# Modulation sums of two half-matrices kept in one PSUM bank, gathered by small DMAs and turned by one transpose per vector

## The chip, the core and the metric

The kernel runs on one core of a Trainium2 chip. The core has TensorE (matrix products, PE in the profile), VectorE (DVE), ScalarE (ACT), GpSimd (POOL) and SyncE (SP), an on-chip memory of 128 partitions (SBUF) and a smaller one of eight banks into which TensorE writes (PSUM). Transfers are issued by an engine's queue and carried out by 16 DMA engines. The metric is the time of one execution in microseconds of the device. Three runs of the kernel before gave 1747.1, 1747.19 and 1747.67 us, a median of 1747.19.

## The reference

Two layers of a network on 512 rows of width 1024, in 32-bit floats. Each layer has a mixer (layer 0: a gated recurrence beside gated linear attention; layer 1: a gated delta rule) and a mixture of 32 experts. Around both stands a modulation computed from one vector `c`:

```python
cond = jax.nn.silu(c)
for layer in range(DEPTH):
    mod = cond @ w_ada[layer] + b_ada[layer]
    sh1, sc1, gt1, sh2, sc2, gt2 = jnp.split(mod[:, None, :], 6, axis=-1)
    u = rms_norm(h, norm1[layer]) * (1.0 + sc1) + sh1
    h = h + gt1 * mixer(u)
    u = rms_norm(h, norm2[layer]) * (1.0 + sc2) + sh2
    h = h + gt2 * hier_moe(u, ...)
```

So each layer needs six vectors of 1024 numbers (v = 0 to 5 in the kernel: sh1, sc1, gt1, sh2, sc2, gt2). Each is a product of a vector of 1024 with a matrix of 1024 x 1024, 4 MB of `w_ada`. Vectors 1 and 4 are further increased by one and multiplied with the norm's weights.

## The kernel before

The kernel runs through four stages: the mixer of layer 0 (to about 290 us), its experts (to about 810 us), the mixer of layer 1 (to about 1235 us) and its experts. In the mixers TensorE multiplies weights that ScalarE has split into a high part (`whi`) and GpSimd into a low part (`wlo`), three products for each pair of operands (lines 402 to 404). In the experts, pairs of experts go through TensorE, their weights (1 MB a transfer, issued by SP) in a ring of buffers.

Two vectors of layer 0 (0 and 1) are made at the start by other code, which the change does not touch. The other ten come from `mods` (line 302): six in layer 0's mixer, among them vectors 1 and 0 of layer 1, and four in layer 1's. `mods` is a generator that runs beside the mixer: the class `Stream` counts steps of the mixer's loop, and each `yield n` lets n steps pass (`M0 = 3, 4, 4` steps in layer 0, `M1 = 6` in layer 1). So the modulation's instructions are written between those of the mixer. A scheduler then fixes the order on each engine, mostly as written, and gives the tiles their room and the semaphores.

The matrix of a vector is taken in quarters: two halves of the columns (`hb`), and in each two halves of the rows (`i`), each a transfer of 1 MB by SP. `mod_rows` (line 254) multiplies one quarter: four matmuls, each with one column of `cond` repeated 32 times, write to the four groups of 32 partitions of a PSUM bank, so that each group holds a part of the sum, the same in its 32 rows. ScalarE copies the bank to `modrow` for `i` = 0 (line 337), VectorE adds the bank for `i` = 1 to it (line 333). One step later `finish` makes columns of it: `mod_columns` (line 261) multiplies each of four blocks of 128 columns with a column of `fold`, which adds the four partial sums and puts the result on 128 partitions. That is four matmuls of one column with a weight load of 128 each, twice per vector. `mod_finish` (line 289) adds the bias and, for vectors 1 and 4, the norm's weights, on VectorE. For vectors 3 and 4 the columns are taken in an interleaved order (`spread`, line 42).

Vectors are used as columns in `u_block` (line 519), in the router's product with `wr` (line 1260, started through `then` when vector 3 is done) and by `gate_rows` (line 347). In order of creation the vectors of layer 0's mixer are (0, 2), (0, 4), (0, 3), (0, 5), (1, 1), (1, 0), written as (layer, v); those of layer 1's are (1, 2), (1, 4), (1, 3), (1, 5).

Eight PSUM banks serve all products (`ps`, line 116). The queue of SP issues every transfer of the middle of the program; ScalarE issues three at the start and two at the end.

Of the kernel before, what the change touches and what calls it, by code (L numbers as in the profile page):

```python
# [7 lines left out]
F32 = mybir.dt.float32  # L8
# [4 lines left out]
OP = mybir.AluOpType  # L13
AX = mybir.AxisListType
# [3 lines left out]
P = 128  # L18
# [23 lines left out]
def spread(x, h):  # L42

    return [x[:, c + j:c + 256:2] for c in (512 * h, 512 * h + 256) for j in range(2)]
# [45 lines left out]
class Build:  # L90
# [167 lines left out]
            self.nc.tensor.matmul(p[32 * q:32 * q + 32], self.cond[:, k0 + q:k0 + q + 1].to_broadcast([P, 32]), w[:, q],  # L258
                                  start=start, stop=stop)

    def mod_columns(self, p, rows, spaced=False):

        for j in range(4):
            x = spread(rows, 0)[j] if spaced else rows[:, j * P:(j + 1) * P]
            self.nc.tensor.matmul(p[:, j:j + 1], x, self.fold[:, 0:1], start=True, stop=True)

    def mod_first(self, hb, p):
        nc = self.nc
# [17 lines left out]
                             stop=True)  # L286
        yield p

    def mod_finish(self, l, v, hb, p):

        nc = self.nc
        d = self.mod_vec(l, v)[:, 4 * hb:4 * hb + 4]
        spaced = v in (3, 4)
        b = self.spc[:, :, 4 * l + 2 * (v - 3) + hb] if spaced else self.C("bada", 48 * l + 8 * v + 4 * hb, 4)
        nc.vector.tensor_add(d, p, b)
        if v % 3 == 1:
            g = self.spc[:, :, 8 + 2 * l + hb] if spaced else self.C("norm1", 8 * l + 4 * hb, 4)
            nc.vector.scalar_tensor_tensor(d, d, 1.0, g, op0=OP.add, op1=OP.mult)
        if hb:
            self.ready.add((l, v))  # L300

    def mods(self, vs, pool, ahead, pace, then={}):


        seq = [(l, v, hb, i) for l, v in vs for hb in range(2) for i in range(2)]
        tiles = []

        def issue():
            if len(tiles) < len(seq):
                l, v, hb, i = seq[len(tiles)]  # L310
                src = self.a["w_ada"][l][512 * i:512 * i + 512, v * D + hb * 512:v * D + hb * 512 + 512]
                tiles.append(self.load(src, 512, pool))

        def finish():
            _, l, v, hb, rows = made.pop(0)
            p = self.ps([P, 4])
            self.mod_columns(p, rows, v in (3, 4))
            self.mod_finish(l, v, hb, p)
            if hb and (l, v) in then:
                then[l, v]()  # L320
        for _ in range(ahead):
            issue()
        made = []
        for n, (l, v, hb, i) in enumerate(seq):
            yield pace[n % len(pace)]
            if made and made[0][0] == n:
                finish()
            p = self.ps()
            self.mod_rows(p, tiles[n], 4 * i)
            tiles[n] = None  # L330
            issue()
            if i:
                self.nc.vector.tensor_add(rows, rows, p)
                made.append((n + 1, l, v, hb, rows))
            else:
                rows = self.mix.tile([P, 512], F32, name="modrow", tag="modrow")
                self.nc.scalar.activation(rows, p, AF.Copy)
        for _ in range(len(made)):
            yield 3
            finish()  # L340

    def get(self, l, v):

# [1616 lines left out]
```

## Time and profile before

| | |
|---|---|
| median of three runs | 1747.19 us |
| profiled execution | 1746.73 us, span 1745.0 us |
| mean granted TensorE clock | 0.973 |
| PE busy | 1651.2 us (95%), 9036 records |
| DVE busy | 806.4 us (46%) |
| ACT busy | 518.9 us (30%) |
| POOL busy | 394.8 us (23%) |

The span runs from the first to the last instruction. Busy time is the time in which an engine has at least one instruction in work; TensorE's matmuls overlap, and a 32-bit product of 512 columns has two records. A matmul's weight load has its own line (PEld). The granted clock is 1.0 at TensorE's full speed and 0.5 at half. The time in square brackets behind a row is the engine's idle time just before it, with what ended it.

### The profile page before, as it was taken

The page shows a single profiled execution, that of the slowest core. Times are in us where ns is not written, and L with a number is a line of the kernel's source. Part 1 is how long each engine was busy: PE and PEld are TensorE (multiplying, and loading weights), DVE is VectorE, ACT ScalarE, POOL GpSimd, SP SyncE. Part 2 cuts the span into 40 slices and gives each one's busy share as a digit, 9 for nine tenths or more (in the row PEclk, how much of TensorE's full clock was granted, in tenths as well). Part 3 has the DMA queues.
Part 4 walks back from the last instruction along what each step waited for, and adds up shares of the span by engine and source line. Part 5 has one row for each costly group of instructions (what it writes and reads, how often), then busy time and mean ns, then how long its engine had stood idle before and what let it go on. Part 6 is the DMA issues. An engine that isn't in the chain of part 4 may idle for free. (4 is left out here: it accounts for less than half of the span.)

```text
span 1745.0 us, 23263 instructions
## 1 busy us (share of the span) xinstructions
PE 1651.2 (95%) x9036; PEld 1003.2 (57%) x9036; DVE 806.4 (46%) x1793; ACT 518.9 (30%) x1027; POOL 394.8 (23%) x350
## 2 busy tenths in 40 slices
PE   6999999899999999998988989899999999999996
PEld 3666767544554555454667667678544554555453
DVE  2344653532433233335687787865432433243324
ACT  4745332310110111014636475364310110111013
POOL 2443523210010101001534343353210010101011
PEclk9999999999999999998999999999999999999998
DMA  8655655589999999994243432237599999999992
GB/s 300 223 173 175 217 185 216 221 358 380 413 413 412 413 411 414 411 409 137 63 141 111 132 110 85 85 106 281 226 368 378 413 411 412 413 411 414 412 407 106
DMA packets 156051, 495.89 MB, mean 284 GB/s; under 512 B 16216, under 2 KB 43156, under 8 KB 140576
## 3 DMA queue, kind: packets, MB, share of 16 engines
q1 hardware_dynamic: 155488, 493.23, 73.4%
q8 instruction: 74, 1.21, 0.3%
q10 hardware_dynamic: 448, 1.11, 0.2%
q14 instruction: 41, 0.34, 0.1%
HBM read 492.21 MB, written 2.10 MB: 283 GB/s over the span
## 5 line engine op out<-in xcount | busy, mean ns | idle before, releaser
L1502 PE MATMUL ps<-w,XTm 128*64 128x512 f32 x2048 | 447.2, 593 | 0.0
L1502 PEld LDWEIGHTS ps<-w,XTm 128*64 128x64 f32 x2048 | 161.7, 137 | 267.6 <-issue 260.7
L396 POOL TENSOR_TENSOR wlo<-w,whi 128x512 fp32r<-128x512 f32 x136 | 181.5, 1339 | 269.1 <-ACT whi L395 251.4
L1556 PE MATMUL ps<-w,hT 128*64 128x512 f32 (+1 forms) x1056 | 230.9, 587 | 1.0 <-ACT hT L1534 1.0
L1525 DVE TENSOR_TENSOR gg<-gg,ps 128x512 f32<-128x512 f32 x32 | 22.0, 688 | 377.4 <-PE ps L1502 377.3
L402 PE MATMUL ps<-w,whi 128*128 128x512 f32 x384 | 165.6, 432 | 0.0
L403 PE MATMUL ps<-w,whi 128*128 128x512 f32 x384 | 155.2, 405 | 2.1 <-POOL w L526 1.5
L1556 PEld LDWEIGHTS ps<-w,hT 128*64 128x64 f32 x1056 | 82.2, 137 | 130.2 <-issue 117.5
L404 PE MATMUL ps<-w,wlo 128*128 128x512 f32 x384 | 155.4, 405 | 0.0
L1579 DVE TENSOR_TENSOR w<-w,ps 128x512 f32<-128x512 f32 (+1 forms) x248 | 149.4, 665 | 7.0 <-PE ps L1570 5.5
L1511 POOL CAST sel<-ident 32x128 fp32r<-32x128 f32 x32 | 9.0, 280 | 591.7 <-PE ps L1539 533.9
L1560 POOL TENSOR_TENSOR yl<-y,yh 128x512 fp32r<-128x512 f32 x60 | 76.4, 1274 | 251.3 <-ACT yh L1559 251.3
L1559 ACT ACTIVATE yh<-y 128x512 fp32r<-128x512 f32 (+1 forms) x66 | 40.8, 618 | 295.4 <-DVE y L1558 294.4
L395 ACT ACTIVATE whi<-w 128x512 fp32r<-128x512 f32 x136 | 84.4, 627 | 147.5 <-PE ps L403 81.0
L1426 PE MATMUL ps<-Dm,hhi 128*128 128x256 f32 x512 | 126.2, 288 | 0.0
L1426 PE MATMUL ps<-Dm,hlo 128*128 128x256 f32 x512 | 123.6, 284 | 0.0
L1558 DVE SCALAR_TENSOR_TENSOR y<-ps,wsl,gate 128x512 f32<-128x512 f32 (+1 forms) x66 | 48.5, 735 | 151.5 <-issue 76.3
L1426 PEld LDWEIGHTS ps<-Dm,hhi 128*128 128x128 f32 x512 | 101.5, 199 | 13.4 <-issue 13.3
L1570 PE MATMUL ps<-yh,dt 128*128 128x512 f32 (+1 forms) x264 | 106.0, 406 | 0.0
L1534 ACT ACTIVATE hT<-ps 128x512 f32<-128x512 f32 x32 | 19.1, 598 | 284.2 <-PE ps L1532 265.9
L1426 PEld LDWEIGHTS ps<-Dm,hlo 128*128 128x128 f32 x512 | 101.6, 199 | 0.1
L1570 PE MATMUL ps<-yl,dt 128*128 128x512 f32 (+1 forms) x264 | 100.9, 387 | 0.0
(520 smaller groups left out, 2433.4 us busy)
## 6 DMA issues: line engine op xcount, KB each, us to landing
w<-in_moe_w_dram SPq DMA_DIRECT2D x380, 1024.0 KB, 14.9
w<-in_w_ada_dram SPq DMA_DIRECT2D x40, 1024.0 KB, 5.5
w<-in_w_in_c_dram SPq DMA_DIRECT2D x16, 1024.0 KB, 9.0
w<-in_w_in_ab_dram SPq DMA_DIRECT2D x10, 1024.0 KB
wst<-in_w_ada_dram SPq DMA_DIRECT2D x8, 1024.0 KB, 12.9
w<-in_w_out_ab_dram SPq DMA_DIRECT2D x4, 1024.0 KB, 4.8
w<-in_moe_w_dram SPq DMA_DIRECT2D x8, 512.0 KB, 15.2
w<-in_w_out_c_dram SPq DMA_DIRECT2D x4, 1024.0 KB, 4.9
```

What stands on the lines that cost most here:

```text
L395: nc.scalar.activation(hi, src, AF.Copy)
L396: nc.gpsimd.tensor_sub(lo, src, hi.bitcast(F32))
L402: mm(p, lhs[0], rhs[0], start=start, stop=False)
L403: mm(p, lhs[0], rhs[1], start=False, stop=False)
L404: mm(p, lhs[1], rhs[0], start=False, stop=stop)
L1426: nc.tensor.matmul(p, spread(src[:, t], k // 4)[k % 4], Dm[:, t].rearrange("p e s -> p (e s)"), start=t + i == 0, stop=t == NT - 1 and i == 1)
L1502: self.nc.tensor.matmul(ps[j][half[e]], X[:, k, half[e]], w, start=k == 0, stop=k == KD - 1)
L1556: nc.tensor.matmul(py[half[e]], hT[:, k, half[e]], w, start=k == 0, stop=k == 3)
L1558: nc.vector.scalar_tensor_tensor(y32, py, wsl, gate[:, c], op0=OP.mult, op1=OP.mult)
L1560: (nc.vector if last else nc.gpsimd).tensor_sub(yl[:, c], y32, yh[:, c].bitcast(F32))
L1570: mm = nc.tensor.matmul(p, dt[:, t * P:(t + 1) * P], y[:, s], start=i == 0, stop=i == 1)
L1579: nc.vector.tensor_add(h, h, p)
```

## The change

The sums of both row halves of a column half are now formed in one PSUM bank: `mod_rows` for `i` = 0 starts the bank and for `i` = 1 goes on in it, so the bank is held over one step of the generator, and VectorE's addition is gone. ScalarE copies the bank to `modrow` once, after `i` = 1. Only four of the 128 rows of `modrow` differ (rows 0, 32, 64 and 96). Small transfers, issued by ScalarE, carry these four rows in pieces into a small tile `modst`: 32 rows of 128 numbers for most vectors (four transfers per half), 16 rows of 256 for vectors 3 and 4 (two per half). When both halves are there, one transpose on TensorE (two for vectors 3 and 4) puts the pieces on 128 partitions, one VectorE reduction adds the four partial sums of all eight columns, and the bias and norm operations run once per vector instead of once per half. `finish` is written after the next vector's first `mod_rows`, and what hangs on a finished vector (`then`) one step of the generator later. The number of modulation matmuls and of 1 MB transfers stays.

```diff
@@ -258,11 +258,10 @@
             self.nc.tensor.matmul(p[32 * q:32 * q + 32], self.cond[:, k0 + q:k0 + q + 1].to_broadcast([P, 32]), w[:, q],
                                   start=start, stop=stop)
 
-    def mod_columns(self, p, rows, spaced=False):
+    def mod_columns(self, p, rows):
 
         for j in range(4):
-            x = spread(rows, 0)[j] if spaced else rows[:, j * P:(j + 1) * P]
-            self.nc.tensor.matmul(p[:, j:j + 1], x, self.fold[:, 0:1], start=True, stop=True)
+            self.nc.tensor.matmul(p[:, j:j + 1], rows[:, j * P:(j + 1) * P], self.fold[:, 0:1], start=True, stop=True)
 
     def mod_first(self, hb, p):
         nc = self.nc
@@ -286,18 +285,32 @@
                              stop=True)
         yield p
 
-    def mod_finish(self, l, v, hb, p):
+    def mod_finish(self, l, v, st):
 
         nc = self.nc
-        d = self.mod_vec(l, v)[:, 4 * hb:4 * hb + 4]
-        spaced = v in (3, 4)
-        b = self.spc[:, :, 4 * l + 2 * (v - 3) + hb] if spaced else self.C("bada", 48 * l + 8 * v + 4 * hb, 4)
-        nc.vector.tensor_add(d, p, b)
+        d = self.mod_vec(l, v)
+        n = st.shape[0]
+        if v in (3, 4):
+            p = self.ps([P, 2, n])
+            for j in range(2):
+                nc.tensor.transpose(p[:, j], st[:, j::2], self.ident[:n, :n])
+            src = p.rearrange("p j (h c q) -> p h c j q", h=2, q=4)
+            dst = d.rearrange("p (h c j) -> p h c j", h=2, c=2)
+            b = self.spc[:, :, 4 * l + 2 * (v - 3):4 * l + 2 * (v - 3) + 2].rearrange("p a h -> p h a")
+            g = self.spc[:, :, 8 + 2 * l:8 + 2 * l + 2].rearrange("p a h -> p h a")
+        else:
+            p = self.ps([P, n])
+            nc.tensor.transpose(p, st, self.ident[:n, :n])
+            src = p.rearrange("p (h j q) -> p h j q", h=2, q=4)
+            dst = d.rearrange("p (h j) -> p h j", h=2)
+            b = self.C("bada", 48 * l + 8 * v, 8).rearrange("p (h a) -> p h a", h=2)
+            g = self.C("norm1", 8 * l, 8).rearrange("p (h a) -> p h a", h=2)
+        nc.vector.tensor_reduce(dst, src, axis=AX.X, op=OP.add)
+        d = d.rearrange("p (h a) -> p h a", h=2)
+        nc.vector.tensor_add(d, d, b)
         if v % 3 == 1:
-            g = self.spc[:, :, 8 + 2 * l + hb] if spaced else self.C("norm1", 8 * l + 4 * hb, 4)
             nc.vector.scalar_tensor_tensor(d, d, 1.0, g, op0=OP.add, op1=OP.mult)
-        if hb:
-            self.ready.add((l, v))
+        self.ready.add((l, v))
 
     def mods(self, vs, pool, ahead, pace, then={}):
 
@@ -312,32 +325,47 @@
                 tiles.append(self.load(src, 512, pool))
 
         def finish():
-            _, l, v, hb, rows = made.pop(0)
-            p = self.ps([P, 4])
-            self.mod_columns(p, rows, v in (3, 4))
-            self.mod_finish(l, v, hb, p)
-            if hb and (l, v) in then:
-                then[l, v]()
+            _, l, v, st = made.pop(0)
+            self.mod_finish(l, v, st)
+            if (l, v) in then:
+                after.append(then[l, v])
         for _ in range(ahead):
             issue()
-        made = []
+        made, after = [], []
         for n, (l, v, hb, i) in enumerate(seq):
             yield pace[n % len(pace)]
-            if made and made[0][0] == n:
-                finish()
-            p = self.ps()
-            self.mod_rows(p, tiles[n], 4 * i)
+            if not i:
+                p = self.ps()
+            self.mod_rows(p, tiles[n], 4 * i, not i, i == 1)
             tiles[n] = None
             issue()
+            while after:
+                after.pop()()
+            if made and made[0][0] < n:
+                finish()
             if i:
-                self.nc.vector.tensor_add(rows, rows, p)
-                made.append((n + 1, l, v, hb, rows))
-            else:
                 rows = self.mix.tile([P, 512], F32, name="modrow", tag="modrow")
                 self.nc.scalar.activation(rows, p, AF.Copy)
+                if not hb:
+                    st = self.mod_stack(v)
+
+                m, w = st.shape
+                for j in range(m // 8):
+                    r = m // 2 * hb + 4 * j
+                    self.nc.scalar.dma_start(st[r:r + 4], rows[::32, w * j:w * j + w])
+                if hb:
+                    made.append((n, l, v, st))
         for _ in range(len(made)):
+            yield 4
+            finish()
+        while after:
             yield 3
-            finish()
+            after.pop()()
+
+    def mod_stack(self, v):
+
+
+        return self.mix.tile([16, 256] if v in (3, 4) else [32, P], F32, name="modst%d" % (v in (3, 4)), bufs=1)
 
     def get(self, l, v):
```

On ScalarE, in layer 0's mixer (`modrow` is the copied bank, `modst` the gathered rows, `whi` the high part of mixer weights), it stands so before:

```order
L592 ACTIVATE xc<-ps,cv_167 128x512
L337 ACTIVATE modrow<-ps 128x512
L395 ACTIVATE whi<-w 128x512 x2
L629 ACTIVATE ge<-ps 128x512
L635 ACT_TABLE_LOAD
L635 ACTIVATE ge<-ge 128x512
L337 ACTIVATE modrow<-ps 128x512
```

and now:

```order
L620 ACTIVATE xc<-ps,cv_167 128x512
L348 ACTIVATE modrow<-ps 128x512
L355 DMA modst_600<-modrow 4x128 x4
L423 ACTIVATE whi<-w 128x512 x2
L657 ACTIVATE ge<-ps 128x512
L663 ACT_TABLE_LOAD
L663 ACTIVATE ge<-ge 128x512
```

Four transfers stand behind each copy, ahead of the next weight split; a copy per half has moved, and none is added.

On TensorE at vector (0, 3) and the router's product (`mod_1054`, in the new kernel `mod_1209`, is that vector; `wr` the router's weights; `w,cond` modulation matmuls), before:

```order
L402 MATMUL ps<-w,whi 128x512
L403 MATMUL ps<-w,whi 128x512
L404 MATMUL ps<-w,wlo 128x512
L265 MATMUL ps<-fold,modrow 128x1 x4
L1260 MATMUL ps<-wr,mod_1054 128x36 x4
L258 MATMUL ps<-w,cond 32x512 x4
L402 MATMUL ps<-w,whi 128x512
L1260 MATMUL ps<-wr,mod_1054 128x36 x4
L403 MATMUL ps<-w,whi 128x512
L404 MATMUL ps<-w,wlo 128x512
```

and now (between the pieces stand 15 matmuls of the mixer):

```order
L258 MATMUL ps<-w,cond 32x512
L296 MATMUL ps<-ident,modst_1009 128x16 x2
L430 MATMUL ps<-w,whi 128x512
L431 MATMUL ps<-w,whi 128x512
L432 MATMUL ps<-w,wlo 128x512
...
L432 MATMUL ps<-w,wlo 128x512
L258 MATMUL ps<-w,cond 32x512 x3
L1288 MATMUL ps<-wr,mod_1209 128x36 x8
L430 MATMUL ps<-w,whi 128x512
```

The column matmuls are replaced by two transposes, and the router's product has moved behind the next modulation matmuls.

On TensorE at the last vector of layer 0's mixer, (1, 0), before (`orow` is the attention's output, `whi` and `yBhi` the output projection):

```order
L404 MATMUL ps<-whi,yAlo 128x512
L258 MATMUL ps<-w,cond 32x512 x4
L883 MATMUL ps<-ident,orow 128x128 x4
L265 MATMUL ps<-fold,modrow 128x1 x4
L402 MATMUL ps<-whi,yBhi 128x512
```

and now:

```order
L432 MATMUL ps<-whi,yAlo 128x512
L258 MATMUL ps<-w,cond 32x512 x4
L911 MATMUL ps<-ident,orow 128x128 x4
L303 MATMUL ps<-ident,modst_1936 128x32
L430 MATMUL ps<-whi,yBhi 128x512
```

Four column matmuls have become one transpose; the distance to the modulation matmuls is the same.

## Rows read from the trace of the kernel before

**Rows 1.** Stages: us; busy (count) of PE, PEld, DVE, ACT, POOL; PEclk; DMA; GB/s.

```profile
0.00:44.00 44.00, 27.67 (x163) 15.70 (x164) 13.06 (x37) 17.63 (x26) 10.93 (x17) 1.00 0.83 298
44.00:290.00 246.00, 237.02 (x1215) 165.65 (x1214) 118.46 (x228) 112.85 (x223) 104.59 (x75) 0.94 0.59 202
330.00:780.00 450.00, 448.38 (x2298) 229.82 (x2298) 148.15 (x272) 54.98 (x91) 40.14 (x44) 1.00 0.99 398
830.00:1200.00 370.00, 337.41 (x2235) 258.81 (x2234) 284.50 (x756) 200.46 (x426) 154.75 (x134) 0.96 0.34 115
```

**Rows 2.** Waits of SP, 330 to 780 us: us in total, times, longest.

```profile
SPq L131 <- PE ps L1502: 182.6, 54, 10.6
```

**Rows 3.** Waits of TensorE, 830 to 1200 us, the two largest.

```profile
PE ps L1067 <- ACT vT L986: 5.9, 3, 3.6
PE ps L285 <- DVE xr L281: 5.8, 5, 2.9
```

**Rows 4.** Groups by shape: count | busy us, mean ns | idle before, releaser.

```profile
L265 PE MATMUL ps<-fold,modrow 128*128 128x1 f32 x160 | 22.2, 260 | 3.3 <-DVE modrow L333 3.1
...
L333 DVE TENSOR_TENSOR modrow<-modrow,ps 128x512 f32<-128x512 f32 x20 | 13.6, 680 | 37.1 <-PE ps L258 37.0
```

**Rows 5.** Timeline of TensorE, 68 to 71 us: start, us, instruction.

```profile
68.83 0.95 PE L265 MATMUL ps<-fold,modrow 128*128 128x1 f32 x8
69.64 0.48 PE L402 MATMUL ps<-w,whi 128*128 128x512 f32 x1
```

**Rows 6.** Timeline of TensorE, 116 to 124 us.

```profile
116.35 1.06 PE L258 MATMUL ps<-w,cond 128*32 128x512 f32 x8
...
123.06 0.99 PE L265 MATMUL ps<-fold,modrow 128*128 128x1 f32 x8
123.97 0.64 PE L258 MATMUL ps<-w,cond 128*32 128x512 f32 x4
```

**Rows 7.** Timeline around two stops of TensorE in layer 0.

```profile
105.97 2.33 DVE L622 TENSOR_TENSOR_SCAN xc<-gtba,tanh 128x512 f32<-128x512 f32 x2
108.94 1.23 PE L265 MATMUL ps<-fold,modrow 128*128 128x1 f32 x5 [3.15 <-DVE modrow L333]
...
155.62 4.43 DVE L712 TENSOR_TENSOR_SCAN gcum<-scan,lgx 128x512 f32<-128x512 f32 x2
160.16 1.08 PE L1260 MATMUL ps<-wr,mod 128*128 128x36 f32 x8 [2.50 <-DVE mod L295]
```

**Rows 8.** Stretches after the two stops, columns as in rows 1.

```profile
109.00:114.00 5.00, 5.00 (x19) 3.08 (x20) 2.96 (x6) 1.90 (x4) 1.35 (x2) 0.50 0.07 11
...
162.00:165.50 3.50, 3.50 (x10) 2.68 (x9) 3.50 (x7) 2.25 (x5) 1.67 (x1) 0.51 0.00 0
```

**Rows 9.** Timeline of TensorE, 50 to 52 us.

```profile
50.70 0.65 PE L238 MATMUL ps<-ident,vsp 12*128 12x12 f32 x4
```

**Rows 10.** Timeline of the start: ScalarE's small transfers and who waits.

```profile
1.43 0.33 ACTq L194 DMA_DIRECT2D vst<-in_b_ada_dram  x1
...
1.79 0.44 ACTq L194 DMA_DIRECT2D vst<-in_norm_dram  x1
...
7.14 0.42 PE L204 MATMUL ps<-ident,vst 112*128 112x112 f32 x1 [2.98 <-DMA vst<-in_norm_dram]
```

**Rows 11.** Small transfers of line 194, from issue to landing.

```profile
DMA to landing us min/median/max: 1.8/6.5/11.3
```

**Rows 12.** Timeline of TensorE at the last vector of each layer.

```profile
271.65 1.06 PE L258 MATMUL ps<-w,cond 128*32 128x512 f32 x8
274.80 1.16 PE L883 MATMUL ps<-ident,orow 128*128 128x128 f32 x4 [2.08 <-DVE orow L877]
276.07 1.87 PE L265 MATMUL ps<-fold,modrow 128*128 128x1 f32 x8
...
1101.57 1.06 PE L258 MATMUL ps<-w,cond 128*32 128x512 f32 x8
...
1106.87 0.97 PE L265 MATMUL ps<-fold,modrow 128*128 128x1 f32 x8
```

## The prediction

> **What bounds the kernel now.** I read the busy table by stage first. In the expert stage of layer 0 TensorE is busy for 448 of 450 us, while the DMA engines move 398 GB/s [rows 1]. Which of the two sets the pace is told by the SP queue, which issues the weight loads: its largest wait in that stretch is for TensorE to give a buffer back, 182.6 us in 54 waits [rows 2], and no TensorE wait of that stretch is for a load. So TensorE sets the pace, the loads follow it, and a mixer that ends earlier moves the expert stage forward whole. The change lies in the two mixers. In layer 0 (44 to 290 us) TensorE is busy for 237 of 246 us; in layer 1 (830 to 1200 us) for 337 of 370, with VectorE at 285 [rows 1]. Time taken off TensorE in layer 0 is therefore nearly all time; in layer 1 part of it may turn into waits on VectorE and ScalarE, which already hold TensorE up there, as the two largest show [rows 3].
>
> **What goes.** Twenty groups of four column matmuls against `fold` (line 265) leave TensorE, 12 in layer 0 and 8 in layer 1; the trace has them as 160 records [rows 4]. Their busy sum of 22.2 us overlaps with neighbours, so I take starts: the group at 68.83 holds the next matmul back until 69.64, 0.81 us, and the one at 123.06 the next until 123.97, 0.91 us [rows 5, 6]. At 0.87 us that is 17.4 us: 10.4 in layer 0, 7.0 in layer 1. The twenty adds of line 333 (13.6 us of VectorE [rows 4]) go as well; they are hidden except where a column group waited for one. That happened once by much: VectorE was in a scan when the matmuls were done, and TensorE stood 3.15 us before the group at 108.94 [rows 7]. After it the granted clock is 0.50 from 109 to 114, the 1.2 GHz level [rows 8]: five microseconds at half speed, 2.5 us. The new order has no column group there, so 5.6 us go. A second stop, 2.50 us before the router's product at 160.16, also ends on the modulation vector, which stood behind the two scans of 155.62 [rows 7], and 3.5 us at 0.51 follow it, 1.7 us [rows 8]. In the new order the product stands some 20 matmuls behind the transposes, but the reduction that makes its operand stands behind six more VectorE instructions. I count half of the 4.2 us, 2.1, with 0 and 4.2 as ends.
>
> **What comes.** Six vectors get one transpose and four get two: 14 transposes, 8 in layer 0. Four transposes of 12 rows in a row took 0.65 us [rows 9], 0.16 each; standing alone I take 0.25, so 3.5 us (2.0 and 1.5). The ends are 0.16 and the 0.65 of the whole row: 2.2 and 9.1 us. Ten reductions with their adds stand on VectorE in place of twenty adds of 512 columns, hidden as those were; ScalarE keeps its twenty copies, moved from the first to the second half sum.
>
> The price to settle is the 64 small DMAs that ScalarE issues. Each vector's columns now wait for a transfer. The clock from the last modulation matmul to data in place: some 0.1 us until the copy, 0.6 us of copy, then four issues (two for the interleaved vectors), of which ScalarE's own at the start of the kernel take 0.33 and 0.44 us [rows 10]; so 1.8 us to the start of the last issue (1.1 with two), and then the landing, L. The nearest row for L is the third transfer of ScalarE's queue at the start: issued at 1.79, it releases TensorE at 7.14, 5.35 us later [rows 10]. Then the DMA engines were 0.83 busy; in layer 0's mixer they are 0.59 and in layer 1's 0.34 [rows 1]. I take 4.5. SP's small transfers bound it on both sides, 1.8 to 11.3 us, median 6.5 [rows 11]; those stood behind megabyte loads on their own queue.
>
> Against this stands the time until TensorE reaches the transposes. Mid layer, the matmuls that start at 116.35 are done about 1.06 us later and the columns follow at 123.06, 5.7 us on [rows 6]; the transposes stand behind the next vector's matmuls as well, one more microsecond, so 6.7. With L = 4.5 the data are there after 6.3: no wait for the five vectors like it. The last vector of layer 0 is tight: matmuls at 271.65, done at 272.7, four transposes of the attention at 274.80 after 2.08 us of waiting, the columns at 276.07 [rows 12]. Data that need 6.3 us meet a transpose due after 3.4: 2.9 us of new wait, with nothing to cover it, since the matmuls that follow on TensorE stand behind it in order. Last vector of layer 1: from 1102.6 to 1106.87 it is 4.3 us [rows 12], and the new order puts six more matmuls between, 1.4 us: due after 5.7, wait 0.6. In the rest of layer 1 the steps lie further apart than in layer 0, and I charge nothing. A stop of two microseconds or more has been followed by a lower clock both times above, 1.7 us in the smaller case; I charge 1.6 once.
>
> The Trainium skill, SBUF — State Buffer, section "The DMA setup-cost knee", puts the fixed cost of any transfer at about 2 us; the first row above does not agree, with 5.35 us under load. With 2 us the waits would shrink to 0.4 us and the time would be near 1727 us. The same skill, DMA: Bandwidth & Descriptors, section "Issuing engines are not separate DMA queues", speaks against a second queue as shelter: ScalarE's transfers share the 16 engines with SP's loads; no run here shows it yet.
>
> Three smaller things are set to nothing. The bank that now holds a half's sums for the span of two steps leaves seven for the rest: TensorE's order outside the modulation is nearly unchanged, so I expect none to be missed; ends 0 and 3 us lost. ScalarE spends 64 issues of some 0.38 us, 24 us, beside work that leaves it idle half the time, busy for 113 of 246 and 200 of 370 us [rows 1]; if a weight split behind them is late, TensorE waits; ends 0 and 4 us lost. Against both, VectorE is relieved of 13.6 us, and in layer 1 TensorE waits for VectorE; ends 0 and 3 us gained. Of layer 1's 5.5 us net I strike one for the waits it may uncover.
>
> **Sum.** Layer 0: 10.4 - 2.0 + 5.6 + 2.1 - 2.9 - 1.6 = 11.6. Layer 1: 7.0 - 1.5 - 1.0 - 0.6 = 3.9. Together 15.5 us. The profiled execution took 1746.73 us with a span of 1745.0; the median of the three runs is 1747.19, 0.5 us more. The sum is taken off the span and so off either: 1731.2 against the profiled execution, 1731.7 against the median. I predict 1732.
>
> **Rivals.** *The transfers are quick* (L of about 2): waits and the charged clock drop go (5.1 us), the router's stop goes whole (2.1), 1.0 returns in layer 1: gain about 23.5, 1724 us. For it: half-idle DMA engines. Against it: the only row of ScalarE's queue.
>
> *The gain is eaten off the path.* Layer 1's 3.9 us turn into waits on VectorE and ScalarE, the router's stop stays (2.1), the issues on ScalarE and the held bank cost 4 us where splits are late: 15.5 - 10 = 5.5, some 1742, and with the landing of the startup row (waits of 0.5 us at three vectors, 0.9 more at each of the two last ones, 3.3 in all) 1745. For it: layer 1's waits [rows 3]. Against it: layer 0 has hardly any.
>
> *The transposes wait for their rows throughout*: slower. The place is every transpose; TensorE is in order, so all its work stands behind. With L, the waits are L - 4.9 for three vectors, L - 5.6 for the two interleaved ones of layer 0, L - 1.6 and L - 3.9 for the last ones, and 1.6 us of clock for each wait over 2 us. Everything else gains 20.6. At L = 6.5 the loss is 17.3, at 7 it is 25.6: it decides from about 6.7 us. At 7.5 the loss is 29.1 and the time 1756; at 11.3, the slowest small transfer, 1785. For it: the median of 6.5 [rows 11] and megabyte loads in flight all through the mixers. Against it: that median is of transfers queued behind such loads on one queue. It could also come from ScalarE's queue itself: each of its transfers waits for an earlier one to finish, among which are SP's loads.
>
> **Chances.** The forecast, 1727 to 1738: 0.55. Quick transfers: 0.15. Eaten: 0.19, half of it under 1743.7. Slower: 0.11. The measurement cannot tell 0.2%, about 3.5 us, from no change. Faster: 0.55 + 0.15 + 0.10 = 0.80; within: 0.10; slower: 0.10. The range for 8 in 10 reaches from 1722 to 1745.
>
> **What would show it.** Right: no column matmuls of 1 column; no stop near 100 us; TensorE's wait for a transposed stack of rows found at the end of layer 0's mixer and hardly elsewhere; the span shorter by some 11 us at the first expert stage and by 15 at the end. Wrong: several waits of TensorE for the small transfers, more stretches at half clock, ScalarE held on its queue with the weight splits behind it late, or a layer 1 mixer no shorter than before.

## The result, and the profile after

The changed kernel took 1736.18 us in the median of four runs (1732.64 to 1737.35), the kernel before 1747.14 beside it: a ratio of 0.9936, 95% interval 0.9924 to 0.9948. The forecast was 1732, with a range of 1722 to 1745. So the time came out 4 us above the forecast, and 11 of the 15.5 us were gained. By the experiments below, the waits for the small transfers cost more than twice what the forecast gave them, and the columns' replacement gains no time without the sums. One execution of the kernel before, of 1969.34 us at a granted clock of 0.80, is left out of all that follows.

The profiled execution is the shortest of the four, 1732.64 us with a span of 1730.8. Three stages of it, columns as in rows 1:

```profile
44.00:290.00 246.00, 233.61 (x1181) 158.28 (x1180) 112.96 (x215) 116.49 (x235) 106.65 (x76) 0.96 0.60 207
330.00:780.00 450.00, 448.38 (x2282) 228.80 (x2282) 147.16 (x269) 55.07 (x91) 42.71 (x46) 1.00 0.99 399
830.00:1200.00 370.00, 340.21 (x2193) 258.44 (x2188) 284.08 (x754) 207.73 (x443) 154.75 (x135) 0.96 0.38 128
```

Against [rows 1], TensorE is busy for less of the first mixer although the stretch now holds more of the program, the expert stage is what it was, and the second mixer looks alike. When the same TensorE instruction is looked up in both traces, the new one is ahead by 1.2 us at 44 us, 9.3 at 289, 8.4 at 360, still 8.3 at 812, 13.0 at 1200 and 14.4 from 1290 to the end. The lead of the mixers is carried through the expert stages, as forecast.

What holds TensorE up in layer 0 (30 to 290 us; us in total, times, longest):

```profile
PE ps L303 <- DMA modst<-modrow: 4.8, 1, 4.8
PE ps L296 <- DMA modst<-modrow: 3.0, 1, 3.0
PE ps L911 <- DVE orow L905: 2.0, 1, 2.0
```

The stop before the columns and the one before the router's product [rows 7] are gone. Two waits for small transfers have come: one at the last vector, forecast at 2.9 us, and one of 3.0 us that was not forecast. The second is at vector (0, 3). The timeline of all engines there (chosen rows; start, us, instruction, idle before):

```profile
144.24 1.06 PE L258 MATMUL ps<-w,cond 128*32 128x512 f32 x8
144.64 0.57 ACT L348 ACTIVATE modrow<-ps 128x512 f32<-128x512 f32 x1
145.25 1.04 ACTq L355 DMA_DIRECT2D modst<-modrow  x2
145.37 0.37 SPq L134 DMA_DIRECT2D w<-in_w_ada_dram  x1
146.84 1.04 PE L258 MATMUL ps<-w,cond 128*32 128x512 f32 x2
150.85 0.37 PE L296 MATMUL ps<-ident,modst 16*128 16x16 f32 x2 [2.97 <-DMA modst<-modrow]
```

The modulation's matmuls free the buffer of their matrix quarter, and SP issues the next 1 MB load into it at 145.37, between the two small transfers. By the semaphore events of the trace the small one issued at 145.25 landed after 1.62 us, the one issued at 145.78 after 4.83. And TensorE reached the transposes 2.6 us after the product was done, not 6.7. The last vector of layer 0 (chosen rows):

```profile
258.88 1.06 PE L258 MATMUL ps<-w,cond 128*32 128x512 f32 x8
260.00 7.14 SPq L131 DMA_DIRECT2D w<-in_moe_w_dram  x5
260.64 2.26 ACTq L355 DMA_DIRECT2D modst<-modrow  x4
261.94 1.25 PE L911 MATMUL ps<-ident,orow 128*128 128x128 f32 x4 [2.00 <-DVE orow L905]
265.18 1.26 POOL L917 TENSOR_TENSOR yBlo<-yf,yBhi 128x512 fp32r<-128x512 f32 x1 [4.17 <-ACT yBhi L916]
268.01 0.28 PE L303 MATMUL ps<-ident,modst 32*128 32x32 f32 x1 [4.82 <-DMA modst<-modrow]
268.22 0.79 PE L430 MATMUL ps<-whi,yBhi 128*128 128x512 f32 x1
```

Loads of the experts are in the queue from 260.00 on; the four small transfers landed 5.2 to 5.7 us after their issues. From the start of the last modulation product to the start of the output projection (line 430) it is 9.3 us. In the kernel before it was 6.15, from 271.65 [rows 12] to 277.80 (chosen rows of its timeline, 271 to 280 us):

```profile
277.80 0.77 PE L402 MATMUL ps<-whi,yBhi 128*128 128x512 f32 x1
277.94 1.28 POOL L889 TENSOR_TENSOR yBlo<-yf,yBhi 128x512 fp32r<-128x512 f32 x1 [4.17 <-ACT yBhi L888]
278.80 0.63 PE L404 MATMUL ps<-whi,yBlo 128*128 128x512 f32 x1
```

There the first product with a `yBlo` (line 404) starts before GpSimd has the last `yBlo` ready, at 279.22. So the last `yBlo`, ready at 266.4 in the new kernel, does not explain the stop: the transfer alone does. TensorE's clock over the wait, and over the stretch around it (columns as in rows 1):

```profile
262.50:272.50 10.00, 5.18 (x14) 3.91 (x14) 1.65 (x8) 0.63 (x1) 1.26 (x1) 0.50 1.01 414
263.20:268.00 4.80, 0.00 (x0) 0.03 (x1) 1.14 (x5) 0.63 (x1) 1.26 (x1) 0.50 0.99 411
```

It is at 0.50, 1.2 GHz, from 262.4 to 272.6, through the wait and 4.6 us of work behind it.

**How far transfers take.** Over all 64 small transfers, issue to last semaphore event, by the number of loads (nearly all of 1 MB) that SP issued in the 5.5 us before:

| loads issued before | transfers | shortest | median | longest, us |
|---|---|---|---|---|
| none | 14 | 1.54 | 1.56 | 1.61 |
| one | 23 | 1.61 | 3.69 | 4.93 |
| two | 24 | 3.88 | 4.92 | 5.70 |
| three | 3 | 5.45 | 5.56 | 5.68 |

The median of all is 4.18, near the 4.5 that the forecast took. The fixed cost of about 2 us in the Trainium skill, SBUF — State Buffer, section "The DMA setup-cost knee", is near the first row and a little above it. In the other rows ScalarE's small transfers land later the more loads SP has just issued. The Trainium skill, DMA: Bandwidth & Descriptors, section "Issuing engines are not separate DMA queues", says that transfers run on the same 16 engines and interleave, whichever engine issued them; these rows agree. Each issue on ScalarE costs more than the 0.33 and 0.44 us of [rows 10] (ns, shortest, median and longest):

```profile
L355 ACTq DMA_DIRECT2D modst<-modrow x64: 503/504/1019, 64.9 to 1093.4; - x64
```

**Where the time of a mixer goes.** For the profiled execution of several kernels, the mixer of layer 0 (from the 31st product of `w` with `whi` to the first product of the experts) and what lies between the expert stages. Idle is time without a matmul on TensorE, clock is half of the busy time at granted level 0.5, work is the rest, all in us. The kernels below the first two are those of the experiments. These executions took 1746.73, 1732.64, 1743.63, 1745.51, 1741.40, 1733.66 and 1732.19 us; that of the sums-only kernel is among its longest.

| kernel | layer 0: length | idle | clock | work | layer 1: length | idle | clock | work |
|---|---|---|---|---|---|---|---|---|
| before | 283.1 | 13.5 | 15.7 | 254.0 | 446.2 | 43.9 | 17.9 | 384.4 |
| changed | 274.4 | 17.5 | 9.2 | 247.8 | 441.8 | 41.1 | 19.3 | 381.4 |
| sums only | 279.7 | 9.5 | 16.6 | 253.6 | 446.2 | 43.5 | 17.8 | 384.9 |
| rows only | 285.4 | 23.3 | 14.9 | 247.2 | 445.8 | 46.2 | 21.6 | 377.9 |
| sums, additions put back | 271.9 | 9.2 | 8.1 | 254.7 | 455.1 | 44.5 | 25.4 | 385.2 |
| no transfers | 271.5 | 13.9 | 11.3 | 246.2 | 446.4 | 43.8 | 23.8 | 378.7 |
| two vectors by columns | 269.0 | 10.0 | 9.4 | 249.5 | 448.4 | 45.8 | 22.2 | 380.3 |

The clock column moves from one execution to the next of one kernel, so beside it stands what all runs give. Each run lists its span and mean granted clock; span times (1 - clock) is at most what the throttle took, as it counts idle time too, and the rest is what remains of the span:

| kernel | runs | median us | taken by the clock, mean | rest, mean |
|---|---|---|---|---|
| before | 42 | 1746.5 | 46.9 | 1697.8 |
| changed, both sets | 9 | 1735.8 | 44.1 | 1689.1 |
| sums only | 6 | 1736.8 | 42.8 | 1693.6 |
| rows only | 11 | 1746.2 | 49.8 | 1695.5 |
| sums, additions put back | 11 | 1742.9 | 45.6 | 1696.6 |
| no transfers | 4 | 1730.1 | 41.9 | 1686.7 |
| two vectors by columns | 5 | 1732.3 | 43.6 | 1687.8 |

The rest is the steadier column: within one kernel its standard deviation is 0.8 to 2.4 us, that of the clock column up to 4.4. In the rest the changed kernel gains 8.7 us, the sums alone 4.2, the rows alone 2.3, and the change of the columns on top of the sums 4.5, each with an uncertainty (standard error) below 1 us. Where medians are compared below, part of the difference can be the clock's.

### The profile page after: what moved, and what is told of

Same layout as the page of the kernel before. It is cut to its first block, busy times and chain, and to the rows that moved or that the text cites. A ratio compares the mean times of both kernels' runs of the same rounds, so it can differ in the third digit from the quotient of the medians.

```text
span 1730.8 us, 23035 instructions
## 1 busy us (share of the span) xinstructions
PE 1636.0 (95%) x8890; PEld 980.7 (57%) x8890; DVE 797.8 (46%) x1770; ACT 520.9 (30%) x1029; POOL 397.2 (23%) x350
## 5 line engine op out<-in xcount | busy, mean ns | idle before, releaser
L1454 PEld LDWEIGHTS ps<-Dm,hhi 128*128 128x128 f32 x512 | 101.1, 198 | 13.5 <-issue 13.4
```

Source lines behind the costliest of these rows:

```text
L1454: nc.tensor.matmul(p, spread(src[:, t], k // 4)[k % 4], Dm[:, t].rearrange("p e s -> p (e s)"), start=t + i == 0, stop=t == NT - 1 and i == 1)
```

## The experiments

**The changed kernel again.**

> The changed kernel once more, as a base for the others. Its four times lie at 1732.6 and 1736.0 to 1737.4 us, the profiled one the lowest. Expected: a median of 1735 to 1737, 0.6% under the kernel before, and the same two waits of TensorE for the small transfers, about 3 us near 150 us and about 5 us near 263 us. If the waits were chance, they would stand elsewhere or be gone.

1735.56 us (1728.65 to 1737.32, five runs), ratio 0.9937 (0.9924 to 0.9950), with waits of 3.0 and 4.9 us at the same two places. They belong to the kernel. The two sets together spread over 9 us. Their profiled executions, 1732.64 and 1728.65, differ in the clock, which took 43.3 and 39.7 us: among others it is at half level for 10.2 us near 262 in the first and 6.8 in the second, and for 3.4 us each at 245 and 344 in the first alone.

**The transfers left out.**

```diff
-                for j in range(m // 8):
-                    r = m // 2 * hb + 4 * j
-                    self.nc.scalar.dma_start(st[r:r + 4], rows[::32, w * j:w * j + w])
...
+        self.nc.gpsimd.memset(s, 0.0)
```

Here `s` is the new `modst` tile.

> The 64 small transfers are left out and the transposes read a stack of zeros, so the ten vectors hold only bias and norm. Theory (the transfers cost by their landing, at two places): the waits of 4.8 and 3.0 us go, with some 2 us of half clock after them, so about 1727 us (1724 to 1730). Rival one (the 34 us of issues on ScalarE make weight splits late throughout): 1722 or less. Rival two (the waits hide other waits that come due instead): 1734 or more.

1730.12 us (1727.52 to 1733.66), ratio 0.9898 (0.9883 to 0.9913): 5.7 us under the changed kernel where the theory said 9. Waits of TensorE in layer 0 (here and below 48 to 322 us, the largest; one of 4.5 us near 310, which the changed kernel has too, is left out):

```profile
PE ps L430 <- POOL wlo L423: 2.5, 2, 1.9
PE ps L910 <- DVE orow L904: 2.0, 1, 2.0
PE ps L258 <- DMA w<-in_w_ada_dram: 1.8, 1, 1.8
PE ps L812 <- DVE orow L904: 1.7, 2, 1.2
```

Both waits for transfers are gone and others have come: idle falls only from 17.5 to 13.9 us. TensorE arrives earlier at what GpSimd, VectorE and the loads still owe it. So without any transfer 5.7 us go in the median, of which 2.4 stand in the rest; the ten small tiles that GpSimd sets to zero instead are in this kernel alone.

**The transfers from SP, ahead of the load.**

```diff
-            issue()
+            if not i:
+                issue()
...
-                    self.nc.scalar.dma_start(st[r:r + 4], rows[::32, w * j:w * j + w])
+                    self.nc.sync.dma_start(st[r:r + 4], rows[::32, w * j:w * j + w])
+                issue()
```

> The same small transfers, issued by SP ahead of the 1 MB load that the same matmuls set free, instead of by ScalarE beside it. Theory (a small transfer takes 1.6 us with no load ahead of it and 3 to 5.6 us behind one or two): the transfers of the vector whose wait was 3.0 us land in some 2 us and that wait goes; at the last vector of layer 0 one expert load stays ahead, so of 4.8 us some 2 to 3 stay. SP's loads start 2 to 3 us later, which the slack of the mixer should hide. Time about 1731 us (1729 to 1734). Rival (the landing is a matter of ScalarE's queue or of the number of transfers): landings of 4 to 5 us as before and both waits unchanged, 1736; if the late loads are felt, 1738 or more.

1736.07 us (1733.17 to 1742.55), ratio 0.9947 (0.9933 to 0.9961). The last vector of layer 0 (chosen rows):

```profile
263.07 0.60 ACT L349 ACTIVATE modrow<-ps 128x512 f32<-128x512 f32 x1 [0.35 <-PE ps L258]
263.69 2.16 SPq L356 DMA_DIRECT2D modst<-modrow  x4
265.97 2.07 SPq L131 DMA_DIRECT2D w<-in_moe_w_dram  x4
267.10 0.21 PE L303 MATMUL ps<-ident,modst 32*128 32x32 f32 x1 [0.99 <-DMA modst<-modrow]
```

With the loads behind them the four transfers landed in 1.54 to 1.57 us in place of 5.2 to 5.7, and those of (0, 3) in 1.62. So at these two places the landing goes by the loads ahead and not by the queue. At another vector of this kernel a transfer on the same queue, issued 1.0 and 0.6 us behind two loads, took 7.2 us, and TensorE still waits 4.2 us for transfers in layer 0 (7.8). The time did not move. SP is held while it waits for the copy, 18.8 us in five waits in layer 0, and idle time elsewhere grew: 15.2 us in layer 0 (17.5), but 45.9 between the expert stages (41.1).

**The transposes later.**

```diff
-            if made and made[0][0] < n:
+            if i and made and made[0][0] < n:
...
-            yield 4
+            yield 8
```

> The transposes are written one quarter of a matrix later, behind the next vector's second modulation product instead of its first, and at the end of each mixer eight steps after the last product instead of four. The transfers are unchanged. Theory (only the distance between transfer and transpose was short): both waits go, with the half clock behind them, 1728 us (1725 to 1731). Rival (what uses the vectors comes due first, the router's product or the first block of the next stage): the waits turn up there, 1735 or more.

1737.85 us (1733.75 to 1746.52), ratio 0.9946 (0.9933 to 0.9959). Waits in layer 0, in the longest of the six executions, which is the profiled one:

```profile
PE ps L303 <- DMA modst<-modrow: 4.9, 1, 4.9
PE ps L813 <- DVE orow L905: 3.0, 1, 3.0
PE ps L432 <- POOL wlo L424: 2.1, 2, 1.7
```

The wait at (0, 3) went; in its place TensorE waits longer for the attention's output and for low parts. The last vector could not move: the mixer runs its generator out before the stage ends. A miss of the theory.

**The sums alone, and the rows alone.** The first keeps one bank per half and one copy, and makes columns as before; the second keeps two banks and VectorE's addition, and takes the transfers and transposes.

```diff
sums only, against the kernel before
-            p = self.ps()
-            self.mod_rows(p, tiles[n], 4 * i)
+            if not i:
+                p = self.ps()
+            self.mod_rows(p, tiles[n], 4 * i, not i, i == 1)
...
-                self.nc.vector.tensor_add(rows, rows, p)
...
rows only, against the changed kernel
-            if not i:
-                p = self.ps()
-            self.mod_rows(p, tiles[n], 4 * i, not i, i == 1)
+            p = self.ps()
+            self.mod_rows(p, tiles[n], 4 * i)
...
+                self.nc.vector.tensor_add(rows, rows, p)
...
```

> Only the first part of the change: both row halves of a half summed in one PSUM bank, one copy by ScalarE, no addition by VectorE; the columns are made as in the kernel before, four matmuls of one column against the summing vector per half, twice per vector, no small transfers, no transposes. Theory (the columns' matmuls are the larger part of the gain, the addition cost only the stop near 106 us and its half clock): the 17 us of column matmuls stay, 5.6 us go with that stop and perhaps 2 more at the router's product, so 1740 us (1738 to 1743). Rival (a bank held over a step makes others wait): 1747 or more.

> Only the other part: two banks per half, copy of the first and VectorE's addition of the second as in the kernel before, but then the small transfers and one or two transposes per vector in place of the column matmuls. Theory: the columns' 17 us less 2 to 3.5 for transposes go, the stop near 106 us goes too since no column group stands there, the two waits for transfers come and are about 1 us longer, since the transfers start behind VectorE's addition instead of ScalarE's copy: 1738 us (1735 to 1741). Rival (the sums are the larger part): 1743 or more.

Sums alone: 1736.83 us (1734.21 to 1744.09), ratio 0.9946 (0.9930 to 0.9963). Rows alone: 1746.2 (1744.55 to 1751.62), ratio 1.0004 (0.9994 to 1.0013). In the medians it is the other way round than the theory had it: the sums alone bring about 10 us (6.5 to 12 by the interval) where it gave them 7, the columns' replacement alone nothing. How the gain of the whole change divides is less clear. The six times of the sums-only kernel lie at 1734 to 1738 and, twice, at 1744, and half of its mean gain in span, 4.1 of 8.3 us, is the clock's. In the rest the sums alone bring 4.2 of the 8.7 us, and the columns' replacement on top of them 4.5. Two lines bear on what each part does alone. In the sums-only kernel the column group that stood 3.15 us [rows 7] starts with no stop (timeline of TensorE):

```profile
101.98 0.99 PE L265 MATMUL ps<-fold,modrow 128*128 128x1 f32 x8
```

and in the rows-only kernel TensorE waits, in layer 0:

```profile
PE ps L303 <- DMA modst<-modrow: 11.5, 2, 7.5
```

There, too, the work on TensorE fell as forecast, by 6.8 and 6.5 us, 13.3 in all (the forecast's 17.4 less 3.5 was 13.9); in the changed kernel's execution it fell by 6.2 and 3.0. But the transfers start behind VectorE's addition, and 11.5 us in layer 0 and 1.7 in layer 1 are waited for them: 13.2 us. What the columns gave was paid back in full there.

**The additions put back.** Against the sums-only kernel:

```diff
+                spare = self.mix.tile([P, 512], F32, name="spare", tag="spare", bufs=1)
+                self.nc.vector.tensor_add(spare, rows, p)
```

> The sums-only kernel (one bank per half, one copy, columns as before), with twenty additions of 128x512 put back on VectorE; each reads the bank and writes a spare tile that nothing reads, so VectorE has its 13.6 us again, and no column group waits for it. Theory (the gain of the sums is the wait of the column group for an addition behind a scan, and what follows it): the gain stays, median 1736 to 1739, as without the additions (1736.8). Rival (VectorE's relief of 13.6 us is the gain): it falls back to 1743 to 1747.

1742.86 us (1738.24 to 1749.6), ratio 0.9989 (0.9975 to 1.0003). More than half of the gain of the sums went, 3.0 us of it in the rest and 2.8 in the clock, though no column group waits for an addition and the stops stay away (9.2 us idle in layer 0, against 13.5 before). So in this kernel twenty additions whose results nobody reads are not free. What their price is, the run does not part: VectorE's time, or the bank, which is held over a step as in the sums-only kernel and now also until VectorE has read it. The trace has one short wait for such a bank in layer 1, and a longer one there for VectorE's `xr` (6.6 us in the sums-only kernel; TensorE, 786 to 1240 us):

```profile
PE ps L285 <- DVE xr L281: 8.9, 5, 3.6
PE ps L1184 <- DVE spare L337: 0.3, 1, 0.3
```

**One transfer per half; the same from SP; and with the last vector earlier.** From SP means ahead of the freed load, as above.

```diff
one transfer per half
...
-                for j in range(m // 8):
-                    r = m // 2 * hb + 4 * j
-                    self.nc.scalar.dma_start(st[r:r + 4], rows[::32, w * j:w * j + w])
+                self.nc.scalar.dma_start(st[m // 2 * hb:m // 2 * hb + m // 2], rows[::32])
the last vector earlier
-M0, M1 = (3, 4, 4), (6,)
+M0, M1 = (3, 4, 4, 3, 4, 4, 3, 4, 4, 3, 4, 4, 3, 4, 4, 3, 4, 4, 3, 4, 3, 3, 3, 3), (6,)
```

> The changed kernel with one small transfer per half instead of four (or two): 20 instead of 64, the four rows cut into pieces by the transfer itself, and the reduction reads the pieces in the other order. Theory (landing from the last issue, 0.54 us for each issue): the last vector's wait of 4.9 us falls by 1.6 to 3.3; the 3.0 us wait near 150 us goes, since the only transfer now starts before the load that delayed its second one; ScalarE gets 24 us of issues back. Time about 1732 us (1730 to 1734). Rival (landing grows with what a transfer carries, or the gains come back as other waits): 1735 or more.

> One small transfer per half, issued by SP ahead of the load that the same matmuls set free. SP is then held at the copy for some 1.2 us instead of 3 to 4 with four transfers. Theory: landing of 1.6 to 2 us, waits for transfers at the last vector under 1 us and none near 150 us; the four-transfer version from SP gave back its gain by loads that came late, which should shrink with the shorter hold: 1731 us (1729 to 1734). Rival (any hold of the load queue costs what the landing gains): 1735 or more.

> The changed kernel with the last vector of layer 0's mixer some steps earlier (3, 3, 3, 3 steps between its four quarters instead of 4, 3, 4, 4): 27 matmuls, some 6.5 us, now stand between its last product and its transpose. The vector (0, 3) is as it was. Theory (the wait of 4.9 us was one of distance): it goes, the wait near 150 us stays, 1732 us (1730 to 1734). Rival (the attention's output comes from VectorE no earlier, and TensorE waits for that or for the low parts from GpSimd instead): 1735 or more.

> Both at once: one transfer per half, issued by SP ahead of the freed load, and the last vector of layer 0 at the earlier pace. Alone, the first gave 1734.5. Theory: the 2.9 us that stayed at the last vector go too, 1732 us (1730 to 1734). Rival (waits are passed on): 1734 to 1736.

One transfer: 1735.83 us, ratio 0.9937 (0.9924 to 0.9950). From SP: 1734.54, 0.9929 (0.9916 to 0.9942). Earlier alone: 1734.7, 0.9928 (0.9914 to 0.9941). Both: 1737.61, 0.9951 (0.9937 to 0.9965). All four intervals overlap the changed kernel's. Waits in layer 0 with one transfer, and with the earlier vector:

```profile
PE ps L303 <- DMA modst<-modrow: 3.9, 1, 3.9
PE ps L429 <- POOL wlo L422: 2.7, 2, 1.9
```

```profile
PE ps L911 <- DVE orow L905: 3.7, 1, 3.7
PE ps L296 <- DMA modst<-modrow: 3.1, 1, 3.1
PE ps L814 <- DVE orow L905: 1.9, 1, 1.9
```

With 20 issues in place of 64, ScalarE has 22 us more (44 times 0.50) and the kernel is no faster: the issues are hidden, as forecast. With the vector earlier its wait of 4.8 us is gone, and the wait for the attention's output has grown from 2.0 to 3.7 us. The rivals that spoke of waits passed on were right for one transfer; from SP and with the earlier vector the times lie between theory and rival, and both at once lie above even the rival's 1736.

**Two vectors by columns.** (0, 3) and (1, 0), the two in `OLD`, go without transfers, the other eight as in the changed kernel.

```diff
...
+                if (l, v) in OLD:
+                    st = st + [rows] if hb else [rows]
+                    if hb:
+                        made.append((n, l, v, st))
+                    continue
...
```

> The changed kernel, but two of the ten vectors, (0, 3) and (1, 0), at which TensorE waited 3.0 and 4.9 us, get their columns by four matmuls per half from the copied bank, without transfers. Four groups of 0.87 us come back, two or three transposes of 0.3 us go. Theory (the waits are the price of the transfers at these two): 1736 less 7.9 plus 2.8 is 1731; leaving out all transfers gave only 5.8 us of such waits back, so 1732.5 (1730 to 1735). Rival (TensorE then waits for others as long): 1735 or more.

1732.29 us (1731.96 to 1734.86), ratio 0.9924 (0.9911 to 0.9938), as expected: 3.5 us under the nine runs of the changed kernel in the median, though the two intervals overlap, and 1.3 us under them in the rest, with a standard error of 0.7. Waits in layer 0:

```profile
PE ps L932 <- DVE orow L926: 2.0, 1, 2.0
PE ps L834 <- DVE orow L926: 1.1, 2, 0.6
PE ps L453 <- POOL wlo L445: 1.0, 1, 1.0
```

Idle falls from 17.5 to 10.0 us, and work rises by 1.7. Of the kernels that leave nothing out it has the lowest median.

## Why the prediction was right, and where it was wrong

- *A shorter mixer is kept by the experts.* Right: the lead is 8.4 us at 360 and 8.3 at 812. The signs named were some 11 us at the first expert stage and 15 at the end; 8.4 and 14.4 came.
- *The columns' matmuls, 17.4 us less 3.5.* Their size was right where it was tested alone, 13.3 us of work in the rows-only kernel; in the changed kernel's one execution it is 9.2. Their worth depends on the sums: without them it is paid back by waits for the transfers.
- *The stop near 106 and its half clock, 5.6 us, and the router's stop.* Both went, with the sums alone too.
- *The additions are "hidden except where a column group waited for one".* Not borne out: put back without anybody to wait for them, they took some 6 us in the median and 3.0 in the rest, where the forecast had named only 0 to 3 us for VectorE's relief and took nothing. That they cost as much in the kernel before is not shown: there the sums alone gain 4.2 us in the rest, and the two stops [rows 7] stand for 5.65.
- *No wait at five vectors.* Failed at (0, 3): 3.0 us. The 6.7 us between product and transpose were read at one vector and given to all; at this one they were 2.6. The order shown ahead of the prediction has the transposes there in the middle of the next four modulation matmuls.
- *The last vector, 2.9 us.* It was 4.8: landings of 5.2 to 5.7 us for 4.5, and four issues at 0.54 us or more each from start to start. The last vector of layer 1, forecast at 0.6, did not wait; its transfers met no load and landed in 1.6 us.
- *Layer 1, 3.9 us.* The lead grew by 4.7 there to 1200 us, and by 6.1 to 1290.
- *Layer 0, 11.6 us.* The lead grew by 8.1 between 44 and 289 us. The 3.0 us at (0, 3) and the 1.9 us more at the last vector are larger than the 3.5 us that are missing.

With the waits as measured, 7.8 us for 3.5, the forecast's own sum gives 15.5 - 4.3 = 11.2 us, and 11.0 were gained. So the waits for the transfers are the term that was clearly mis-sized: the landings were longer than the 4.5 us taken at the last vector, and the distance at (0, 3) was shorter than the one read elsewhere. That the rest of the sum then fits so closely is in part luck: in the profiled execution the work on TensorE fell by 9.2 us where the forecast had 13.9, the price of the additions was put at nothing, and the clock, which took 2.8 us less in the mean of nine executions, moves by more than that between single ones. Of the rivals, part of "the gain is eaten off the path" came true: a stop that is removed in layer 0 comes back in part as waits for VectorE and GpSimd. The rival by which the transposes wait throughout did not: two of ten vectors waited. Left open are what an addition costs that nobody waits for, how the gain divides between the sums and the columns, and why the clock of one kernel differs between executions.

## What to carry to other kernels

Price a gather by small transfers by the loads that its own producer sets free: here it landed in 1.6 us with no load ahead, and in 3.7 and 4.9 us in the median behind one and two, and the matmuls that made the data also released the buffer for the next load. Measure the distance from data to first use at every place, not at one, and try the old way where it is short; here the kernel that does so has the lowest median, though not clear of the noise. And take the parts of a change apart before saying which one paid, in the steady part of the time and not in medians alone: here the small-looking part, one accumulating bank in place of an addition, brought 4 of 9 us by the first and about 10 of 11 by the second, and the columns' replacement brought no time without it.

## What the runs showed of the hardware

A transfer of four rows between places on the chip landed in 1.54 to 1.61 us when no load had been issued for 5.5 us (14 cases), the same transfer in 5.45 to 5.68 behind three loads of 1 MB (three cases). One transfer of 16 pieces of 512 or eight of 1024 bytes took 1.70 to 1.81 us in the six cases without a load, hardly more than one of four pieces.

For one and the same kernel the granted clock took between 39.7 and 46.8 us of the span in nine executions, and 38.1 to 48.8 in six of the sums-only kernel, while the rest of the span varied by a standard deviation of 1.5 and 1.7 us. So a single profiled execution of this kernel can be off by 4 us and more, where the whole effect was 11.
